# Two-layer hybrid trunk: the next layer's modulation moved from accumulations on DVE, ACT and POOL to float32r products on PE, and two sets of transpositions issued one tile later

## The chip, the core and the metric

The kernel runs on one core of a Trainium2 chip. The metric is the device time of one execution in microseconds; for each kernel the median of three runs is given. One further execution was taken by the hardware profiler, and all rows below come from that one. The engines are named as in the profile: PE (matrix products; PEld is its loading of weights), DVE (vector), ACT (scalar), POOL (GpSimd) and SP, whose queue issues nearly all transfers.

## What is computed

Two layers of a trunk are run over nine tiles of 128 tokens: one tile of context and eight latent tiles. Cut to what matters here:

```python
mod = jax.nn.silu(c) @ w_ada[l] + b_ada[l]          # for c_ctx and for c: two rows of 3 x 1024
shift, scale, gate = jnp.split(mod, 3, axis=-1)
h = rms_norm(x, p['norm_pre']) * (1 + scale) + shift
u = h @ p['w_in']                                   # 1024 -> 2952 columns: four branches and their gates
qa = rms_norm(gq, p['gqa_q_norm']); ka = rms_norm(gk, p['gqa_k_norm'])   # GQA, then rotary on both
cq = rms_norm(mcq, p['mla_q_norm']); ckv = rms_norm(mckv, p['mla_kv_norm'])   # MLA
...                                                 # attention A and C, scans B and D
y = x + gate * rms_norm(concat(o_a, o_b, o_c, o_d) @ p['w_out'], p['norm_post'])
```

The modulation of a layer is a product of two vectors with a matrix of 1024 x 3072. Everything is float32. A large product is made of three float32r products: both operands are split into a rounded part (`hi`) and the rest (`lo`), and hi x hi, hi x lo and lo x hi are added up in PSUM.

## The kernel before, in words

A layer runs through its projections first, one group of columns after another: LV, SM, MG, XBC, GQA, MLA, the second MLA projection (UQ) and QK. `proj_tok` (SM, GQA, MLA) loads eight slices of weights with `load_w` (a transfer into `wst`, a rounding cast to `whi` on DVE, a subtraction to `wlo` on POOL) and then gives each of the nine token tiles 24 products into one PSUM tile `psP`, of which there are four. `proj_T` (MG, XBC, QK) has columns as output rows, three stretches of 384 tokens each. After each tile `consume` is called: for GQA (`cons_gqa`) ACT squares, DVE reduces, POOL makes the reciprocal root, DVE scales (which frees `psP`), POOL and DVE apply the rotary factors, and PE transposes the result `r` into `gT`, which ACT copies out. `cons_mla` does the like with `z` and `mT`.

Within layer 0's projections a generator, `ada_steps`, makes the modulation that is still missing: the gate of layer 0 and shift, scale and gate of layer 1, as eight halves of 512 columns. A half takes eight steps, one for each 128 rows of `w_ada`; 72 calls of `next(steps_[0])` spread them over the projections from SM to QK. Layer 1 has the same projections without any such steps. Before the change a step loads 128 x 512 weights into `ast` (two buffers) and adds them, times one number for each partition, into `acc`, once for each of the two conditioning vectors: on DVE as one instruction (L176), or for one vector of a gate half on ACT (`pr`) and POOL (L174). PE then adds up the partitions of `acc`: with `acc` as weights and a 2-column `pick` as moving operand for shift and scale (L189), or the other way round for the gate (L183). `acc` has one buffer.

The order of instructions on each engine is not that of the code. A scheduler goes through the program with a model of time and lets each engine take what the model holds to be ready; each engine then runs its list strictly in that order and waits where the model was wrong.

Of the kernel before, what the change touches and what calls it, by code (L numbers as in the profile page):

```python
# [8 lines left out]
F32 = mybir.dt.float32  # L9
# [25 lines left out]
def hybrid_trunk_kernel(ctx: ExitStack, tc: tile.TileContext, a):  # L35
# [35 lines left out]
    dve.tensor_tensor(out=cch[:, :, 2:4], in0=cc, in1=cch[:, :, 0:2], op=ALU.subtract)  # L71
    sel = const.tile([4, 2], F32, name="sel")
    sp.dma_start(out=sel, in_=a["sel"])
# [3 lines left out]
    pool.memset(zero, 0.0)  # L77
    pick = const.tile([128, 2, 2], F32, name="pick")
    pool.memset(pick, 0.0)
    for r in range(2):  # L80
        pool.memset(pick[:, r, r:r + 1], 1.0)
    ident = const.tile([128, 128], F32, name="ident")
# [64 lines left out]

    def ada_rows(p, k, hi, lo):
        pe.matmul(p[0:4, :], lhsT=cch[:, k, :], rhs=hi, start=(k == 0), stop=False, skip_group_check=True)
        pe.matmul(p[0:2, :], lhsT=cch[:, k, 0:2], rhs=lo, start=False, stop=False, skip_group_check=True)  # L150

    def ada_put(mod, half, part, ac, sc, l):
        p = psD("adaT")
        for k in range(4):
            pe.matmul(p[:, 2 * k:2 * k + 2], lhsT=mod[:, k * 128:(k + 1) * 128], rhs=sel, start=(k == 0), stop=(k == 3),
                      skip_group_check=True)
        ada_cols(p, half * 4, 4, part, ac, sc, l)

    def ada_steps(l, parts, wpool, ac, sc, d_gate):

        for part, half in parts:
            o = part * D + half * 512
            acc = wpool.tile([128, 2, 512], F32, name="acc", tag="acc", bufs=1)
            for k in range(KD):
                st = wpool.tile([128, 512], F32, name="ast", tag="ast", bufs=2)
                sp.dma_start(out=st, in_=a["w_ada"][l, k * 128:(k + 1) * 128, o:o + 512])
                for r in range(2):
                    c = cc[:, k, r:r + 1]
                    if k == 0:
                        act.activation(out=acc[:, r, :], in_=st, func=AF.Identity, scale=c)  # L170
                    elif r and part == 2:
                        pr = wpool.tile([128, 512], F32, name="pr", tag="pr", bufs=1)
                        act.activation(out=pr, in_=st, func=AF.Identity, scale=c)
                        pool.tensor_tensor(out=acc[:, r, :], in0=acc[:, r, :], in1=pr, op=ALU.add)  # L174
                    else:
                        dve.scalar_tensor_tensor(out=acc[:, r, :], in0=st, scalar=c, in1=acc[:, r, :], op0=ALU.mult, op1=ALU.add)  # L176
                yield
            p = psC("ada")
            if part == 2:
                gr = wpool.tile([2, 512], F32, name="gr", tag="gr", bufs=1)  # L180
                sp.dma_start(out=gr, in_=a["b_ada"][l, o:o + 512].partition_broadcast(2))
                for r in range(2):
                    pe.matmul(p[0:2, :], lhsT=pick[:, r, :], rhs=acc[:, r, :], start=(r == 0), stop=(r == 1), skip_group_check=True)  # L183
                dve.tensor_tensor(out=gr, in0=p[0:2, :], in1=gr, op=ALU.add)
                sp.dma_start(out=d_gate[:, half * 512:half * 512 + 512], in_=gr)
            else:
                for k in range(4):
                    for r in range(2):
                        pe.matmul(p[:, 2 * k:2 * k + 2], lhsT=acc[:, r, k * 128:(k + 1) * 128], rhs=pick[:, r, :],  # L189
                                  start=(k + r == 0), stop=(k + r == 4), skip_group_check=True)  # L190
                ada_cols(p, half * 4, 4, part, ac, sc, l)
            yield

# [75 lines left out]
    def proj_tok(l, hh, hl, wpool, off, n, consume, rows=iter(())):  # L269
        ws = [load_w(a["w_in"][l, k * 128:(k + 1) * 128, off:off + n], n, wpool) for k in range(KD)]  # L270
        next(rows, None)
        next(rows, None)
        for t in range(T):
# [12 lines left out]
    def proj_T(l, hh, hl, wpool, off, nct, consume, after=None):  # L286
# [92 lines left out]
    for l in range(L):  # L379
# [83 lines left out]
        with st1:  # L463
# [134 lines left out]
            def cons_gqa(t, p):  # L598
# [52 lines left out]
            def cons_mla(t, p):  # L651
# [23 lines left out]
                pool.tensor_tensor(out=kr, in0=kr, in1=r[:, 0:32], op=ALU.add)  # L675
                tp = psD("mT")
                pe.transpose(tp[:, 0:128], z[:, 0:128], ident)
                pe.transpose(tp[0:64, 128:256], z[:, 128:192], ident)
                pe.transpose(tp[:, 256:384], z[:, 192:320], ident)
                s = slice(t * 128, (t + 1) * 128)  # L680
                act.copy(c1h[:, s], tp[:, 0:128])
                dve.tensor_tensor(out=c1l[:, s], in0=tp[:, 0:128], in1=c1h[:, s], op=ALU.subtract)
                act.copy(c2s[0:64, s], tp[0:64, 128:256])
                dve.tensor_tensor(out=c2s[64:128, s], in0=tp[0:64, 128:256], in1=c2s[0:64, s], op=ALU.subtract)
                s = slice(kt * 128, (kt + 1) * 128)
                act.copy(ckh[:, s], tp[:, 256:384])
                dve.tensor_tensor(out=ckl[:, s], in0=tp[:, 256:384], in1=ckh[:, s], op=ALU.subtract)

# [663 lines left out]
def _constants(np):  # L1352
# [16 lines left out]
    def rope(rot):  # L1369
# [17 lines left out]
        "bm": (hd[:, None] == (np.arange(256) // 64)[None, :]).astype(np.float32),  # L1387
        "sel": np.tile(np.eye(2, dtype=np.float32), (2, 1)),
        "hm": (hd[:, None] == np.arange(4)[None, :]).astype(np.float32),
# [91 lines left out]
```

## Time and profile before

| | |
|---|---|
| three runs, median | 1841.7 us (1835.44 to 1841.74) |
| the profiled execution | 1836.28 us, its span 1834.5 us |
| busy in the span | PE 1718.5, PEld 1312.8, DVE 1177.2, ACT 859.9, POOL 729.2 us |
| PE clock granted, mean | 0.973 of full speed |
| layer 0's projections, SM to QK | 102.68 to 423.20 us |
| layer 1's projections, SM to QK | 1014.58 to 1296.20 us |

Times inside the trace count from the first instruction. Busy time of PE is the time in which at least one product is under way, and products overlap, so it says little about how much PE could still take; the distance between two starts says more. The two stretches at the end of the table hold the same projections of the two layers; they begin at the first product of SM (128x296) and end at the first product of the attention that follows (L1102).

### The profile page before, as it was taken

The page shows a single profiled execution, that of the slowest core. Times are in us where ns is not written, and L with a number is a line of the kernel's source. Part 1 is how long each engine was busy: PE and PEld are TensorE (multiplying, and loading weights), DVE is VectorE, ACT ScalarE, POOL GpSimd, SP SyncE. Part 2 cuts the span into 40 slices and gives each one's busy share as a digit, 9 for nine tenths or more (in the row PEclk, how much of TensorE's full clock was granted, in tenths as well). Part 3 has the DMA queues.
Part 4 walks back from the last instruction along what each step waited for, and adds up shares of the span by engine and source line. Part 5 has one row for each costly group of instructions (what it writes and reads, how often), then busy time and mean ns, then how long its engine had stood idle before and what let it go on. Part 6 is the DMA issues. An engine that isn't in the chain of part 4 may idle for free.

```text
span 1834.5 us, 25155 instructions
## 1 busy us (share of the span) xinstructions
PE 1718.5 (94%) x8200; PEld 1312.8 (72%) x8200; DVE 1177.2 (64%) x2297; ACT 859.9 (47%) x1907; POOL 729.2 (40%) x909
## 2 busy tenths in 40 slices
PE   8999998998998998999999999999999899899998
PEld 2787977896665666656887999889666666565676
DVE  5738887647877886772453447543776788678223
ACT  4634422434654765673442162132465467567322
POOL 3633149824343543330343323871434354333011
PEclk9999988999989999999999999999998999999999
DMA  8435353413323321142433333231442332114243
GB/s 296 138 117 156 113 168 103 129 63 119 115 77 85 90 79 47 41 144 86 138 129 104 102 94 91 60 102 37 122 116 76 81 88 83 50 36 149 87 137 115
DMA packets 179684, 190.99 MB, mean 104 GB/s; under 512 B 29406, under 2 KB 140720, under 8 KB 179552
## 3 DMA queue, kind: packets, MB, share of 16 engines
q1 hardware_dynamic: 174208, 179.11, 32.1%
q10 hardware_dynamic: 5344, 10.26, 1.7%
q8 instruction: 65, 1.06, 0.3%
q14 instruction: 67, 0.55, 0.1%
HBM read 141.00 MB, written 48.30 MB: 103 GB/s over the span
## 4 chain that ended last, share of the span: by engine, by line
PE 54%; DVE 17%; DMA 11%; POOL 7%; issue 5%; ACT 4%; SPq 1%; ACTq 0%; POOLq 0%; DVEq 0%
PE psP L267 19%; PE op L267 8%; PE st L1102 5%; PE po L1118 5%; DMA ast<-in_w_ada_dram 2%; PE mx L755 2%; DMA wst<-in_w_in_dram 2%; DVE mx L756 2%; DVE Pl L1110 2%; PE po L1114 1%; DVE acc L176 1%; DMA R<-d_rec 1%; POOL wlo L261 1%; DVE d_DT L1023 1%; PE go L931 1%
## 5 line engine op out<-in xcount | busy, mean ns | idle before, releaser
L756 DVE TENSOR_REDUCE mx<-mx 128x1 f32<-128x512 f32 (+2 forms) x400 | 224.6, 582 | 92.2 <-PE mx L755 90.6
L267 PE MATMUL psP<-whi,hh 128*128 128x512 f32 (+2 forms) x576 | 202.6, 363 | 6.1 <-DVE whi L257 3.7
L267 PE MATMUL psP<-wlo,hh 128*128 128x512 f32 (+2 forms) x576 | 202.8, 361 | 2.1 <-POOL wlo L261 1.9
L267 PE MATMUL psP<-whi,hl 128*128 128x512 f32 (+2 forms) x576 | 187.5, 359 | 0.1
L261 POOL TENSOR_TENSOR wlo<-wst,whi 128x512 fp32r<-128x512 f32 (+3 forms) x106 | 130.6, 1240 | 137.9 <-DVE whi L257 79.0
L267 PE MATMUL psP<-hh,whi 128*128 128x384 f32 x480 | 163.1, 340 | 4.7 <-DVE whi L257 3.8
L1102 PE MATMUL st<-QA,KA 128*128 128x512 f32 (+1 forms) x336 | 164.0, 488 | 0.6 <-DVE Pl L1110 0.4
L267 PE MATMUL psP<-hl,whi 128*128 128x384 f32 x480 | 160.2, 336 | 0.0
L267 PE MATMUL psP<-hh,wlo 128*128 128x384 f32 x480 | 155.0, 337 | 0.1
L1110 DVE TENSOR_TENSOR Pl<-st,Ph 128x512 fp32r<-128x512 f32 x160 | 109.7, 686 | 65.9 <-ACT st L1108 64.2
L1107 ACT ACTIVATE Ph<-st 128x512 fp32r<-128x512 f32 x160 | 95.5, 597 | 107.5 <-PE st L1102 99.1
L1117 ACT ACTIVATE P<-st 128x512 f32<-128x512 f32 (+1 forms) x176 | 99.8, 567 | 79.1 <-PE st L1102 67.1
L1102 PE MATMUL st<-QB,KB 66*128 66x512 f32 (+3 forms) x336 | 133.0, 401 | 0.0
L267 PEld LDWEIGHTS psP<-whi,hh 128*128 128x128 f32 x576 | 110.3, 193 | 20.3 <-DVE whi L257 5.2
L267 PEld LDWEIGHTS psP<-wlo,hh 128*128 128x128 f32 x576 | 110.4, 193 | 17.9 <-POOL wlo L261 5.3
L267 PEld LDWEIGHTS psP<-whi,hl 128*128 128x128 f32 x576 | 108.5, 192 | 12.4 <-DVE hl L226 0.3
L1102 PEld LDWEIGHTS st<-QA,KA 128*128 128x128 f32 x336 | 65.4, 195 | 49.8 <-issue 39.3
L267 PEld LDWEIGHTS psP<-hh,whi 128*128 128x128 f32 x480 | 90.1, 188 | 12.0 <-DVE whi L257 5.5
L1102 PE MATMUL st<-QB,KA 96*128 96x512 f32 (+1 forms) x168 | 93.2, 555 | 2.1 <-ACT P L1117 1.8
L1108 ACT ACTIVATE st<-st 128x512 f32<-128x512 f32 x160 | 94.8, 592 | 0.0
L1118 PE MATMUL po<-P,vm 128*65 128x512 f32 (+1 forms) x176 | 88.7, 586 | 5.9 <-ACT P L1117 3.4
L1144 POOL TENSOR_TENSOR gt<-gt,R 128x512 f32<-128x512 f32 (+1 forms) x24 | 26.6, 1106 | 166.0 <-DMA R<-d_rec 162.3
(369 smaller groups left out, 4325.2 us busy)
## 6 DMA issues: line engine op xcount, KB each, us to landing
ast<-in_w_ada_dram SPq DMA_DIRECT2D x96, 256.0 KB
wst<-in_w_in_dram SPq DMA_DIRECT2D x64, 256.0 KB
wost<-in_w_out_dram SPq DMA_DIRECT2D x16, 512.0 KB
d_xs<-d_xb SPq DMA_DIRECT2D x32, 192.0 KB
ot<-d_oT SPq DMA_DIRECT2D x18, 320.0 KB
d_tok<-vv SPq DMA_DIRECT2D x18, 256.0 KB
d_gt<-gg SPq DMA_DIRECT2D x24, 192.0 KB
g_qk<-d_qk SPq DMA_DIRECT2D x36, 128.0 KB
```

What stands on the lines that cost most here:

```text
L176: dve.scalar_tensor_tensor(out=acc[:, r, :], in0=st, scalar=c, in1=acc[:, r, :], op0=ALU.mult, op1=ALU.add)
L261: eng.tensor_tensor(out=lo[:, 0:n], in0=st[:, 0:n], in1=hi[:, 0:n], op=ALU.subtract)
L267: pe.matmul(p, lhsT=lt, rhs=rh, start=(first and i == 0), stop=(last and i == n - 1))
L755: pe.matmul(p[:, 0:n], lhsT=lt_m[:, s], rhs=rh_m[:, o:o + n], start=True, stop=True)
L756: dve.tensor_reduce(out=mx[:, t, i:i + 1], in_=p[:, 0:n], axis=AX.X, op=ALU.max)
L1102: anchors["pe"] = pe.matmul(sp_[:, 0:nq], lhsT=kx[:, ks], rhs=qx[:, qs], start=(i == 0), stop=(i == len(spasses) - 1))
L1107: act.activation(out=Ph[:, 0:nq], in_=sp_[:, 0:nq], func=AF.Exp, scale=scale)
L1108: anchors["act"] = act.activation(out=sp_[:, 0:nq], in_=sp_[:, 0:nq], func=AF.Exp, scale=scale)
L1110: anchors["dve"] = dve.tensor_tensor(out=Pl[:, 0:nq], in0=sp_[:, 0:nq], in1=Ph[:, 0:nq], op=ALU.subtract)
L1117: anchors["act"] = act.activation(out=P[:, 0:nq], in_=sp_[:, 0:nq], func=AF.Exp, scale=scale)
L1118: pe.matmul(po[0:65, 0:nq], lhsT=v[:, kt, vi, :], rhs=P[:, 0:nq], start=(j == 0), stop=last, skip_group_check=True)
L1144: pool.tensor_tensor(out=g[:, 0:nq], in0=g[:, 0:nq], in1=R[:, 0:nq], op=ALU.mult)
```

## The change

A step of `ada_steps` now splits the 128 x 512 weights: ACT rounds them to `ahi`, DVE or POOL (in turn) subtracts to `alo`, and PE multiplies both with the conditioning vectors as weights of 4 and 2 columns, adding up in one PSUM tile over the eight steps (`ada_rows`, L145 and L146 of the new kernel). The products of a step are issued one step later. A half ends with a copy of the four rows to `mod` on ACT, and one step later with four small float32 products (`adaT`, shift and scale) or one float32 product of 512 columns (gate, L181, in which a fifth row adds the bias). `acc`, `pr`, `pick` and their sums are gone. In `proj_tok`, what `consume` returns is called one tile later; `cons_gqa` and `cons_mla` return the transpositions and the copies behind them.

```diff
@@ ada_steps
-            acc = wpool.tile([128, 2, 512], F32, name="acc", tag="acc", bufs=1)
+            p = psC("ada")
+            behind = None
             for k in range(KD):
                 st = wpool.tile([128, 512], F32, name="ast", tag="ast", bufs=2)
                 sp.dma_start(out=st, in_=a["w_ada"][l, k * 128:(k + 1) * 128, o:o + 512])
-                for r in range(2):
-                    c = cc[:, k, r:r + 1]
-                    if k == 0:
-                        act.activation(out=acc[:, r, :], in_=st, func=AF.Identity, scale=c)
-                    elif r and part == 2:
-                        pr = wpool.tile([128, 512], F32, name="pr", tag="pr", bufs=1)
-                        act.activation(out=pr, in_=st, func=AF.Identity, scale=c)
-                        pool.tensor_tensor(out=acc[:, r, :], in0=acc[:, r, :], in1=pr, op=ALU.add)
-                    else:
-                        dve.scalar_tensor_tensor(out=acc[:, r, :], in0=st, scalar=c, in1=acc[:, r, :], op0=ALU.mult, op1=ALU.add)
+                hi = wpool.tile([128, 512], F32R, name="ahi", tag="ahi", bufs=2)
+                act.copy(hi, st)
+                lo = wpool.tile([128, 512], F32R, name="alo", tag="alo", bufs=2)
+                (pool if k % 2 else dve).tensor_tensor(out=lo, in0=st, in1=hi, op=ALU.subtract)
+                if behind:
+                    ada_rows(p, *behind)
+                behind = k, hi, lo
                 yield
-            p = psC("ada")
+            ada_rows(p, *behind, True)
+
+            mod = wpool.tile([5, 512], F32, name="mod", tag="mod", bufs=1)
+            act.copy(mod[0:4, :], p[0:4, :])
             if part == 2:
...
+                sp.dma_start(out=mod[4:5, :], in_=a["b_ada"][l:l + 1, o:o + 512])
+            yield
+            if part == 2:
+                p = psC("ada")
+                pe.matmul(p[0:2, :], lhsT=sel, rhs=mod, start=True, stop=True)
+                act.copy(mod[0:2, :], p[0:2, :])
+                sp.dma_start(out=d_gate[:, half * 512:half * 512 + 512], in_=mod[0:2, :])
             else:
...
+                ada_put(mod[0:4], half, part, ac, sc, l)
@@ proj_tok
-            consume(t, p)
+
+            last, rest = rest, consume(t, p)
+            if last is not None:
+                last()
             for _ in range(2 - t % 2):
                 next(steps_[0], None)
+        if rest is not None:
+            rest()
@@ cons_gqa (cons_mla alike)
-                tp = psD("gT")
-                for i in range(3):
-                    pe.transpose(tp[:, i * 128:(i + 1) * 128], r[:, i * 128:(i + 1) * 128], ident)
-                act.copy(qT[:, :, t * 128:(t + 1) * 128], tp[:, 0:256].rearrange("p (a b) -> p a b", b=128))
-                act.copy(kT[:, kt * 128:(kt + 1) * 128], tp[:, 256:384])
+
+                def rest():
+                    tp = psD("gT")
+                    ...
+                return rest
```

The order of the built programs differs only between the first tiles of SM and the start of the attention in layer 0: on PE the first 356 and the last 4887 instructions are the same, one for one, by what they do, layer 1's projections with their transpositions among them.

The first place is DVE at the start of GQA in layer 0. `whi` are the casts of GQA's weights, `yc` the end of XBC's convolution, `ss` the reductions of the first two GQA tiles, from which their scaling `z` comes. Before:

```order
L122 SCALAR_TENSOR_TENSOR ac<-ac,np_c 128x8
L176 SCALAR_TENSOR_TENSOR acc<-ast,cc,acc 128x512
L578 SCALAR_TENSOR_TENSOR yc<-xpad,yc 128x1156
L257 CAST whi<-wst 128x512
L176 SCALAR_TENSOR_TENSOR acc<-ast,cc,acc 128x512 x2
L257 CAST whi<-wst 128x512
L176 SCALAR_TENSOR_TENSOR acc<-ast,cc,acc 128x512 x10
L606 TENSOR_REDUCE ss_2429<-sq 128x6
L606 TENSOR_REDUCE ss_2487<-sq 128x6
L609 TENSOR_TENSOR z<-psP,ss_2429 128x384
```

And now:

```order
L574 SCALAR_TENSOR_TENSOR yc<-xpad,cw,yc 128x1156 x2
L250 CAST whi<-wst 128x512
L167 TENSOR_TENSOR alo<-ast,ahi 128x512
L250 CAST whi<-wst 128x512
L577 SCALAR_TENSOR_TENSOR yc<-xpad,yc 128x1156
L605 TENSOR_REDUCE ss_2509<-sq 128x6
L605 TENSOR_REDUCE ss_2569<-sq 128x6
L608 TENSOR_TENSOR z<-psP,ss_2509 128x384
```

Twelve accumulations of the modulation stood around the last cast and ahead of the first reduction; one subtraction is left there, ahead of the last cast.

The second place is PE at the end of QK, the last projection; `mx` are products for the maxima of the attention that follows, `st` its first scores. Before:

```order
L267 MATMUL psP<-hl,whi 128x384
L755 MATMUL mx<-KA_3633,QA_3635 128x256
L267 MATMUL psP<-hh,wlo 128x384
L183 MATMUL ada<-acc,pick 2x512
L1102 MATMUL st<-QA_3635,KA_3633 128x128
L1102 MATMUL st<-QB_3636,KB_3634 128x128
L755 MATMUL mx<-KA_3633,QA_3635 128x512 x2
```

And now:

```order
L260 MATMUL psP<-hh,wlo 128x384
L762 MATMUL mx<-KA_3797,QA_3799 128x512
L145 MATMUL ada<-ahi,cch 4x512
L146 MATMUL ada<-alo,cch 2x512
L1109 MATMUL st<-QA_3799,KA_3797 128x128
L1109 MATMUL st<-QB_3800,KB_3798 128x128
L762 MATMUL mx<-KA_3797,QA_3799 128x256
L181 MATMUL ada<-mod,sel 2x512
```

The last pair of the modulation has come into PE's list, and its closing product (L181, where L183 stood) has moved behind the first scores of the attention.

## Rows read from the trace of the kernel before

**Rows 1.** The profile's page: busy time, share of the span and instructions of PE.

```profile
PE 1718.5 (94%) x8200; PEld 1312.8 (72%) x8200; DVE 1177.2 (64%) x2297; ACT 859.9 (47%) x1907; POOL 729.2 (40%) x909
```

**Rows 2.** Layer 0's projections by stretch: us, busy PE, PEld, DVE, ACT, POOL, clock.

```profile
102.68:136.10 33.42, 31.70 (x221) 29.57 (x220) 14.05 (x29) 12.36 (x30) 13.55 (x12) 1.00 0.45 130
136.10:231.56 95.46, 90.66 (x509) 83.47 (x508) 77.56 (x113) 43.72 (x72) 28.47 (x36) 1.00 0.47 138
231.56:297.01 65.45, 61.23 (x278) 50.07 (x277) 55.10 (x70) 13.97 (x34) 40.01 (x37) 0.92 0.47 137
297.01:349.80 52.79, 46.77 (x268) 43.39 (x267) 33.13 (x62) 20.21 (x81) 45.59 (x76) 0.90 0.35 102
349.80:423.20 73.40, 73.18 (x391) 64.81 (x390) 42.29 (x77) 25.74 (x59) 30.02 (x30) 1.00 0.30 94
sum 320.52, PE 303.55 PEld 271.31 DVE 222.12 ACT 116.00 POOL 157.65; mean PE 60.71 PEld 54.26 DVE 44.42 ACT 23.20 POOL 31.53
```

**Rows 3.** The same five stretches in layer 1, and their sum.

```profile
1014.58:1044.00 29.42, 29.42 (x217) 29.38 (x217) 8.10 (x24) 5.23 (x18) 6.98 (x10) 1.00 0.26 77
1044.00:1130.70 86.70, 86.16 (x497) 82.35 (x496) 50.92 (x78) 38.50 (x64) 18.92 (x29) 1.00 0.31 95
1130.70:1182.60 51.90, 51.50 (x237) 42.29 (x236) 35.99 (x42) 10.80 (x32) 40.96 (x43) 1.00 0.26 72
1182.60:1224.40 41.80, 39.56 (x250) 37.83 (x249) 19.78 (x53) 13.27 (x69) 29.87 (x63) 1.00 0.29 79
1224.40:1296.20 71.80, 69.88 (x383) 64.58 (x382) 30.41 (x62) 19.39 (x47) 17.30 (x22) 1.00 0.21 66
sum 281.62, PE 276.52 PEld 256.43 DVE 145.21 ACT 87.20 POOL 114.04; mean PE 55.30 PEld 51.29 DVE 29.04 ACT 17.44 POOL 22.81
```

**Rows 4.** Whom PE waited for in layer 0's projections: us in total, times, longest.

```profile
PE gT L629 <- DVE r L626: 4.8, 4, 2.6
PE psP L267 <- DVE whi L257: 4.5, 6, 1.5
PE ada L189 <- DVE acc L176: 3.5, 1, 3.5
PE ada L183 <- DVE acc L176: 2.2, 2, 1.7
```

**Rows 5.** In order of time, DVE and ACT at the start of GQA (start, us).

```profile
255.22 0.50 ACT L604 ACTIVATE sq<-psP 128x384 f32<-128x384 f32 x1
260.54 1.42 DVE L176 SCALAR_TENSOR_TENSOR acc<-ast,cc,acc 128x512 f32<-128x512 f32 x2 [0.87 <-DMA ast<-in_w_ada_dram]
261.87 1.00 DVE L606 TENSOR_REDUCE ss<-sq 128x6 f32<-128x384 f32 x2
```

**Rows 6.** PE in order of time, where products of the modulation stand (start, us).

```profile
26.16 1.05 PE L155 MATMUL adaT<-sel,mod 4*128 4x2 f32 x8
...
38.19 0.39 PE L149 MATMUL ada<-ahi,cch 128*4 128x512 f32 x1
38.42 0.40 PE L267 MATMUL psP<-whi,hh 128*128 128x512 f32 x1
...
300.22 0.95 PE L189 MATMUL ada<-pick,acc 128*128 128x2 f32 x8
...
327.15 1.02 PE L183 MATMUL ada<-acc,pick 128*2 128x512 f32 x2
```

**Rows 7.** What writes `ada` on PE: records, ns min/median/max, first and last start.

```profile
L189 PE MATMUL ada<-pick,acc x64: 165/251/374, 182.4 to 300.9; 128*128 128x2 f32 x64
L183 PE MATMUL ada<-acc,pick x16: 591/592/592, 127.9 to 422.7; 128*2 128x512 f32 x16
```

**Rows 8.** What reads `ast`: records, ns min/median/max, first and last start.

```profile
L176 DVE SCALAR_TENSOR_TENSOR acc<-ast,cc,acc x84: 735/751/1828, 111.0 to 374.1; 128x512 f32<-128x512 f32 x84
L140 DVE TENSOR_TENSOR alo<-ast,ahi x12: 670/691/694, 5.2 to 33.0; 128x512 fp32r<-128x512 f32 x12
```

**Rows 9.** Whom DVE waited for in layer 0's projections.

```profile
DVE acc L176 <- DMA ast<-in_w_ada_dram: 16.1, 18, 2.7
```

More of the change, by code (lines that the diff above doesn't have):

```diff
@@ L71, in hybrid_trunk_kernel @@
     dve.tensor_tensor(out=cch[:, :, 2:4], in0=cc, in1=cch[:, :, 0:2], op=ALU.subtract)
-    sel = const.tile([4, 2], F32, name="sel")
+    sel = const.tile([5, 2], F32, name="sel")
     sp.dma_start(out=sel, in_=a["sel"])
@@ L77, in hybrid_trunk_kernel @@
     pool.memset(zero, 0.0)
-    pick = const.tile([128, 2, 2], F32, name="pick")
-    pool.memset(pick, 0.0)
-    for r in range(2):
-        pool.memset(pick[:, r, r:r + 1], 1.0)
     ident = const.tile([128, 128], F32, name="ident")
@@ L146, in ada0, with ada_rows @@
         return load.ins
-    def ada_rows(p, k, hi, lo):
+    def ada_rows(p, k, hi, lo, last=False):
         pe.matmul(p[0:4, :], lhsT=cch[:, k, :], rhs=hi, start=(k == 0), stop=False, skip_group_check=True)
-        pe.matmul(p[0:2, :], lhsT=cch[:, k, 0:2], rhs=lo, start=False, stop=False, skip_group_check=True)
+        pe.matmul(p[0:2, :], lhsT=cch[:, k, 0:2], rhs=lo, start=False, stop=last, skip_group_check=True)
     def ada_put(mod, half, part, ac, sc, l):
@@ L154, in ada_put @@
         for k in range(4):
-            pe.matmul(p[:, 2 * k:2 * k + 2], lhsT=mod[:, k * 128:(k + 1) * 128], rhs=sel, start=(k == 0), stop=(k == 3),
+            pe.matmul(p[:, 2 * k:2 * k + 2], lhsT=mod[:, k * 128:(k + 1) * 128], rhs=sel[0:4], start=(k == 0), stop=(k == 3),
                       skip_group_check=True)
@@ L166, in ada_steps @@
                 sp.dma_start(out=st, in_=a["w_ada"][l, k * 128:(k + 1) * 128, o:o + 512])
-                for r in range(2):
-                    c = cc[:, k, r:r + 1]
-                    if k == 0:
-                        act.activation(out=acc[:, r, :], in_=st, func=AF.Identity, scale=c)
-                    elif r and part == 2:
-                        pr = wpool.tile([128, 512], F32, name="pr", tag="pr", bufs=1)
-                        act.activation(out=pr, in_=st, func=AF.Identity, scale=c)
-                        pool.tensor_tensor(out=acc[:, r, :], in0=acc[:, r, :], in1=pr, op=ALU.add)
-                    else:
-                        dve.scalar_tensor_tensor(out=acc[:, r, :], in0=st, scalar=c, in1=acc[:, r, :], op0=ALU.mult, op1=ALU.add)
+                hi = wpool.tile([128, 512], F32R, name="ahi", tag="ahi", bufs=2)
@@ L179, in ada_steps @@
             if part == 2:
[L180 to L185, printed above, removed]
-            else:
[L187 to L191, printed above, removed]
@@ L192, in ada_steps @@
-            yield
+                sp.dma_start(out=mod[4:5, :], in_=a["b_ada"][l:l + 1, o:o + 512])
[5 more added lines that the diff above has]
+                sp.dma_start(out=d_gate[:, half * 512:half * 512 + 512], in_=mod[0:2, :])
+            else:
+                ada_put(mod[0:4], half, part, ac, sc, l)
     PARTS = [(p, h) for p in (1, 0, 2) for h in range(2)]
@@ L272, in proj_tok @@
         next(rows, None)
+        rest = None
         for t in range(T):
@@ L626, in cons_gqa @@
                 dve.tensor_tensor(out=r, in0=r, in1=sq, op=ALU.add)
-                tp = psD("gT")
-                for i in range(3):
-                    pe.transpose(tp[:, i * 128:(i + 1) * 128], r[:, i * 128:(i + 1) * 128], ident)
-                act.copy(qT[:, :, t * 128:(t + 1) * 128], tp[:, 0:256].rearrange("p (a b) -> p a b", b=128))
-                act.copy(kT[:, kt * 128:(kt + 1) * 128], tp[:, 256:384])
+                def rest():
+                    tp = psD("gT")
+                    for i in range(3):
+                        pe.transpose(tp[:, i * 128:(i + 1) * 128], r[:, i * 128:(i + 1) * 128], ident)
+                    act.copy(qT[:, :, t * 128:(t + 1) * 128], tp[:, 0:256].rearrange("p (a b) -> p a b", b=128))
+                    act.copy(kT[:, kt * 128:(kt + 1) * 128], tp[:, 256:384])
+                return rest
             proj_tok(l, hh, hl, wp, G_GQA, 512, cons_gqa)
@@ L675, in cons_mla, with rest @@
                 pool.tensor_tensor(out=kr, in0=kr, in1=r[:, 0:32], op=ALU.add)
[L676 to L687, printed above, removed]
+                def rest():
+                    tp = psD("mT")
+                    pe.transpose(tp[:, 0:128], z[:, 0:128], ident)
+                    pe.transpose(tp[0:64, 128:256], z[:, 128:192], ident)
+                    pe.transpose(tp[:, 256:384], z[:, 192:320], ident)
+                    s = slice(t * 128, (t + 1) * 128)
+                    act.copy(c1h[:, s], tp[:, 0:128])
+                    dve.tensor_tensor(out=c1l[:, s], in0=tp[:, 0:128], in1=c1h[:, s], op=ALU.subtract)
+                    act.copy(c2s[0:64, s], tp[0:64, 128:256])
+                    dve.tensor_tensor(out=c2s[64:128, s], in0=tp[0:64, 128:256], in1=c2s[0:64, s], op=ALU.subtract)
+                    s = slice(kt * 128, (kt + 1) * 128)
+                    act.copy(ckh[:, s], tp[:, 256:384])
+                    dve.tensor_tensor(out=ckl[:, s], in0=tp[:, 256:384], in1=ckh[:, s], op=ALU.subtract)
+                return rest
             proj_tok(l, hh, hl, wp, G_MLA, 352, cons_mla)
@@ L1387, in _constants @@
         "bm": (hd[:, None] == (np.arange(256) // 64)[None, :]).astype(np.float32),
-        "sel": np.tile(np.eye(2, dtype=np.float32), (2, 1)),
+        "sel": np.concatenate([np.eye(2), np.eye(2), np.ones((1, 2))]).astype(np.float32),
         "hm": (hd[:, None] == np.arange(4)[None, :]).astype(np.float32),
```

## The prediction

> **What bounds the kernel now.** I read the page first: PE is busy for 94% of the span [rows 1]. As products overlap, that number does not say that PE is full, so the next view is busy time by stretch. The two layers run the same projections, layer 0 with the modulation's steps among them and layer 1 without. Layer 0 takes 320.52 us and layer 1 281.62 us [rows 2, 3]: the steps cost 38.9 us now. By stretch the difference is 4.0 us in SM, 8.8 in MG and XBC, 13.6 in GQA, 11.0 in MLA and 1.6 in UQ and QK. PEld, whose loads are hidden behind the products, is busy for 256 of 282 us in layer 1, so there PE is close to what it can take. In layer 0 DVE is busy for 222 us, in layer 1 for 145; in GQA PE idles for 4.2 us and in MLA for 6.0, and there alone the granted clock falls, to 0.92 and 0.90 of full speed [rows 2]. The levels are 2.4 and 1.2 GHz, so a mean of 0.92 over 65.45 us is about 10.5 us at the lower one, and 0.90 over 52.79 us as much. The waits that end last there are for `r`, for `whi` and for `acc` [rows 4]. One of them is plain in order of time: ACT has squared the first GQA tile at 255.2 us, but DVE reduces it at 261.9, since accumulations that wait for `ast` stand ahead in its list [rows 5]; the four `psP` tiles stay taken until then.
>
> **What the change takes away.** On PE two kinds of product go. L183 has 16 records and L189 has 64 [rows 7]; the trace lists a float32 product as two records, so these are 8 and 32 instructions. Two records of L183 take 1.02 us and eight of L189 0.95 [rows 6]: 16 x 0.51 = 8.2 us and 64 x 0.119 = 7.6, together 15.8 us of PE's own time. So of the 38.9 us, 38.9 - 15.8 = 23.1 are waits and lost clock. DVE loses 84 accumulations of 0.751 us (63 us), ACT 44 scalings and POOL 28 additions; that alone is worth nothing to the end unless PE waits less.
>
> **What it adds on PE.** A half has eight steps, each with two float32r products of 512 columns: 8 x 8 x 2 = 128. The first layer-0 modulation issues this very form (L149), and the product behind it starts 38.42 - 38.19 = 0.23 us later [rows 6]. That is what one of the 128-column products costs too: only four columns of weights make it no cheaper. 128 x 0.23 = 29.4 us. Four gate halves end with a float32 product of 512 columns, in the form of L183: 4 x 1.02 = 4.1 us. Four halves of shift and scale end with the small products of L155: 4 x 1.05 = 4.2 us [rows 6]. Together 37.7 us, against 15.8 taken away: PE's list grows by 21.9 us.
>
> The Trainium skill bears on the dearest term: "TensorE: Matmul & The Clock Gate", section "Back-to-back issue gap", gives a sustained 131 ns for a 512-column product in a stream with its loads of weights. By it the 128 products would be 16.8 us, an estimate from that page, and the sum 12.6 us smaller. The row shows 0.23 us, so the row is used, and the page's figure gets no chance of its own.
>
> **What it adds elsewhere.** ACT gets 64 roundings and twelve small copies. ACT is busy for 116 of 320 us [rows 2], so this is hidden unless something behind it in ACT's list is due: ACT's casts wait for `ast` now, and the copies and squares that free `psP` are queued behind them. DVE and POOL get 32 subtractions each. DVE's took 0.691 us [rows 8], 22 us in all, so DVE comes out 41 us lighter. POOL's count hardly changes (28 additions gone). SP's transfers of `ast` stay 64, with two buffers; each buffer is now freed by the subtraction. Of the bias, the transfer to two rows becomes one to one row. The last product, L181, has moved behind the attention's first scores and waits for a copy on ACT; I take that into the remainder below.
>
> **The transpositions.** From the attention of layer 0 on PE's list is the same as before, so in layer 1 the later issue moves nothing: it is worth nothing there. In layer 0 the scheduler had placed the transpositions by readiness already. Counting the products between a GQA tile's last one and its `gT`, at their distances between starts, tiles three to nine had 13.5 to 23.5 us before and have 10.8 to 20.8 now: they stand no later, but DVE, which is late with `r`, has less ahead of it. I give this half of the 4.8 us of waits [rows 4], and nothing more.
>
> **The sum.** Layer 0's projections after the change are layer 1's 281.6, plus 37.7 for PE, plus a remainder X of waits beyond those of layer 1. Below, X can be -5.1: layer 1 has 281.62 - 276.52 = 5.1 us of PE idle, which pairs could fill [rows 3]. Above, without new waits, it is the 23.1 of today. By stretch I take 2 of SM's (there the steps follow each other as fast as `ast` arrives, now as before), 2.5 in MG and XBC, 2 in GQA (the block of accumulations is gone, and with it the waiting for `acc` and most of the low clock), 4 in MLA, where `whi` and `r` remain late, nothing in UQ and QK, and -4.5 for holes filled: X = 6, nearer the lower end since DVE, which three of the four waits name, loses 41 us. 281.6 + 37.7 + 6 = 325.3, against 320.5: 4.8 us more. The profiled execution took 1836.28 us, 1.8 more than its span, and becomes 1841.1. It lies 5.4 below the median of the three runs; carried over to the median, 1841.7 + 4.8 = 1846.5 us.
>
> By stretch: SM +3 us, MG and XBC +3, GQA -5, MLA -1, UQ and QK +5. In the last PE is never idle for long (73.18 of 73.40), so eleven pairs come to it as they are.
>
> **The rivals.** A measurement of this kernel can tell about 0.5%, 9.2 us, from no change.
>
> *Holes filled, faster.* The pairs are products that need no `psP` tile, so PE can take them while it waits for one. For a gain of 9.2 us X must fall below -8.0, which means that also waits inside layer 1's pattern go, and no clock is lost. At X = -9 the window takes 310.3 us and the kernel 1831.5. For it: GQA and MLA idle now. Against it: PE's list alone is 319.3 us beside layer 1's. Chance 0.10.
>
> *A wait at each pair, slower.* PE's list has 64 pairs at fixed places, each behind a transfer, a cast and a subtraction, where before PE met the modulation in eight places. DVE waited 16.1 us for `ast` in 18 places, 0.9 us each [rows 9]; if PE's places come as early and nothing fills them, X is 6 + 16 = 22 and the time 1862.5. It decides from X = 10.4 on. For it: an accumulation takes 0.735 to 1.828 us [rows 8], so what the scheduler counts on is missed by up to a microsecond. Against it: one late pair moves PE's whole list, so that the next is no longer early, and DVE has fewer of these instructions. Chance 0.25.
>
> A rule of the Trainium skill speaks for this rival: in "SBUF — State Buffer", section "SBUF: two separate sides", a DVE instruction with two SBUF inputs and one of POOL hold a shared pair of ports in turn, each blocking the other for a whole instruction. Both subtractions of the change are of that kind. The spread of L176 agrees; what an `alo` costs against POOL is in no row.
>
> *The transpositions help nothing.* If `r` stays as late as it is, the 4.8 us and the clock that falls behind them (5.3 us in MLA at half speed) stay: about 6.5 us more than taken, X = 12.5, 1853. For it: the transpositions stand no later than before. Against it: the lighter DVE. Chance 0.13.
>
> *The forecast*, within 9.2 us either way: chance 0.52. Its own range is X from 0 to 10, 1840 to 1851 us.
>
> **Range and chances.** For 8 in 10 I go down to X = -6 (1834.5 us), which leaves out most of the first rival, and up to X = 20 (1860.5), which leaves out the worst of the second: 1834 to 1861 us. Faster by over 0.5% is the first rival, 0.10; slower the second and third, 0.25 + 0.13 = 0.38; within 0.5% the forecast, 0.52.
>
> **What would show it.** Right: DVE busy near 180 us from SM to the first scores instead of 222, PE's pairs 0.23 us apart, GQA shorter than 65.45 us, the last stretch some 5 us longer, the first GQA reduction within a microsecond or two of its square, and everything from the attention on unchanged. Wrong: PE waiting for `alo` or `ahi` for more than 5 us in all; waits for `r` of over 4 us; a clock below 0.95 in GQA or MLA; pairs that cost less than 0.2 us; or a changed time outside this window.

## The result, and the profile after

The changed kernel takes 1855.88 us (median of four runs, 1854.17 to 1857.73), the one before in the same rounds 1839.78: a ratio of 1.0095, with a 95% interval of 1.0072 to 1.0118. It is slower by 0.95%, inside the range that was given and beyond the time that was forecast.

The profiled execution has a span of 1855.4 us, 20.9 more than before. The first view is again busy time by stretch, in the same five stretches of layer 0 (columns as in [rows 2]):

```profile
103.15:139.98 36.83, 35.79 (x240) 31.79 (x239) 9.36 (x27) 12.51 (x32) 9.89 (x10) 1.00 0.49 137
139.98:246.69 106.71, 100.24 (x545) 87.94 (x543) 60.20 (x89) 49.81 (x86) 31.90 (x37) 0.98 0.41 120
246.69:308.49 61.80, 59.44 (x268) 44.84 (x267) 43.42 (x50) 17.91 (x45) 51.70 (x48) 1.00 0.38 109
308.49:363.60 55.11, 50.68 (x290) 44.92 (x289) 26.24 (x61) 21.07 (x84) 40.85 (x72) 0.94 0.42 122
363.60:441.12 77.52, 77.28 (x412) 67.18 (x410) 36.71 (x71) 26.24 (x62) 24.07 (x27) 1.00 0.31 97
sum 337.97, PE 323.43 PEld 276.67 DVE 175.94 ACT 127.54 POOL 158.40; mean PE 64.69 PEld 55.33 DVE 35.19 ACT 25.51 POOL 31.68
```

The window has grown from 320.5 to 338.0 us, by 17.4 of the 20.9. Against [rows 2], SM is 3.4 us longer, MG and XBC 11.3, GQA 3.7 shorter, MLA 2.3 longer, UQ and QK 4.1 longer. DVE is 46 us lighter and the wait for `acc` is gone; GQA now runs at the full clock. The same stretches of layer 1 are where they were, 281.62 then and now:

```profile
sum 281.82, PE 276.51 PEld 256.58 DVE 147.71 ACT 87.15 POOL 114.32; mean PE 55.30 PEld 51.32 DVE 29.54 ACT 17.43 POOL 22.86
```

Whom PE waited for in the window (us, times, longest), to be held against [rows 4]:

```profile
PE psP L260 <- DVE whi L250: 4.5, 6, 1.5
PE ada L145 <- ACT ahi L165: 3.0, 4, 2.0
PE gT L630 <- DVE r L625: 2.4, 2, 2.0
PE psP L260 <- POOL wlo L254: 1.8, 3, 0.9
PE cums L508 <- DVE av L500: 1.2, 1, 1.2
```

At the pairs themselves PE waits 3.0 us in all. The wait for `whi` is what it was, that for `r` has halved, and `wlo` and `av` are new. A pair in order of time (start, us):

```profile
429.75 0.39 PE L145 MATMUL ada<-ahi,cch 128*4 128x512 f32 x1
429.98 0.39 PE L146 MATMUL ada<-alo,cch 128*2 128x512 f32 x1
430.21 0.39 PE L762 MATMUL mx<-KA,QA 128*128 128x512 f32 x1
```

The products of the pairs stand 0.23 us apart; over all 128 the median is 0.234, which makes 30.0 us. The Trainium skill's "TensorE: Matmul & The Clock Gate", section "Back-to-back issue gap", has 131 ns for a 512-column product in a sustained stream; this trace does not agree.

The first GQA tile in order of time:

```profile
269.14 0.50 ACT L603 ACTIVATE sq<-psP 128x384 f32<-128x384 f32 x1
269.68 0.55 DVE L605 TENSOR_REDUCE ss<-sq 128x6 f32<-128x384 f32 x1 [4.28 <-ACT sq L603]
```

DVE now reduces half a microsecond after the square, where it came 6.65 us after it [rows 5]. The longest wait for `r` comes later, at one of GQA's last tiles, with MLA's weights being made ready (PE, DVE, POOL and SP together, start in us):

```profile
310.99 1.23 SPq L248 DMA_DIRECT2D wst<-in_w_in_dram  x2
313.37 0.34 DVE L250 CAST whi<-wst 128x352 fp32r<-128x352 f32 x1 [2.71 <-DMA wst<-in_w_in_dram]
313.63 0.95 DVE L618 TENSOR_TENSOR r<-z,ropes 128x384 f32<-128x384 f32 x1
314.12 1.26 POOL L254 TENSOR_TENSOR wlo<-wst,whi 128x352 fp32r<-128x352 f32 x1
314.96 0.62 DVE L250 CAST whi<-wst 128x352 fp32r<-128x352 f32 x1
315.34 1.36 POOL L167 TENSOR_TENSOR alo<-ast,ahi 128x512 fp32r<-128x512 f32 x1
315.50 1.61 DVE L625 TENSOR_TENSOR r<-r,sq 128x384 f32<-128x384 f32 x1
317.17 0.55 PE L630 MATMUL gT<-ident,r 128*128 128x128 f32 x3 [1.97 <-DVE r L625]
```

This shows how PE comes to wait. A cast waits 2.71 us for its weights with `r` queued behind it, and then the last step of `r` takes 1.61 us, beside a subtraction `alo` on POOL; the one of the tile before took 0.55. A slow step of this kind is not new, though: in the kernel before it took up to 1.63 us. PE waits 1.97 us for it, and its clock falls:

```profile
157.00:160.50 3.50, 3.50 (x14) 2.90 (x13) 0.21 (x2) 0.95 (x3) 0.00 (x0) 0.53 0.33 112
316.50:324.50 8.00, 7.33 (x27) 6.31 (x28) 2.53 (x7) 1.78 (x4) 6.13 (x7) 0.57 0.58 176
```

These two are nearly all of the window's time at 1.2 GHz: 2 x (1 - 0.53) x 3.5 + 2 x (1 - 0.57) x 8 = 10.2 us, half of the 21 before.

That the `alo` beside it is what stretches `r` is what the Trainium skill would have, in "SBUF — State Buffer", section "SBUF: two separate sides": DVE with two SBUF inputs and POOL take turns on a shared pair of ports, each for a whole instruction. The row agrees, with 1.06 us; one pair of rows does not show that it is the port.

### The profile page after: what moved, and what is told of

Same layout as the page of the kernel before. It is cut to its first block, busy times and chain, and to the rows that moved or that the text cites. A ratio compares the mean times of both kernels' runs of the same rounds, so it can differ in the third digit from the quotient of the medians.

```text
span 1855.4 us, 25323 instructions
## 1 busy us (share of the span) xinstructions
PE 1741.0 (94%) x8288; PEld 1318.6 (71%) x8288; DVE 1133.2 (61%) x2241; ACT 872.7 (47%) x1939; POOL 729.4 (39%) x910
## 4 chain that ended last, share of the span: by engine, by line
PE 33%; DVE 7%; DMA 5%; POOL 3%; issue 2%; ACT 2%; SPq 0%; ACTq 0%; POOLq 0%; DVEq 0%
PE psP L260 12%; PE op L260 9%; PE st L1109 3%; PE po L1125 2%; PE mx L762 1%; DVE mx L763 1%; DMA R<-d_rec 1%; POOL ss L103 1%; PE po L1121 1%; POOL sq L621 1%; DVE Pl L1117 1%; DMA wst<-in_w_in_dram 1%; PE go L938 1%; PE po L1119 0%; PE po L1120 0%
## 5 line engine op out<-in xcount | busy, mean ns | idle before, releaser
L250 DVE CAST whi<-wst 128x512 fp32r<-128x512 f32 (+3 forms) x114 | 72.7, 650 | 50.9 <-DMA wst<-in_w_in_dram 33.4
```

Source lines behind the costliest of these rows:

```text
L250: dve.tensor_copy(hi[:, 0:n], st[:, 0:n])
```

## The experiments

Two theories were set against each other. **List**: PE's list has grown by 21.9 us, and that is what arrives. **Chain**: what arrives comes from feeding the pairs, 64 times a transfer, a rounding and a subtraction, whose places in the lists of SP, ACT, DVE and POOL delay what the projections need. Beside them stood the question what the later transpositions are worth. "Window" is the time of the five stretches in the one profiled execution of a kernel; ratios are to the kernel before, in the same rounds on the same chip (its median was 1839.8 us in the changed kernel's rounds and 1836.0 to 1837.6 in those of the others, so medians of different rows are compared by their ratios).

| kernel | window, us | median, us | ratio, 95% interval |
|---|---|---|---|
| before | 320.5 | 1839.8 | |
| changed | 338.0 | 1855.9 | 1.0095 [1.0072, 1.0118] |
| e1, modulation only | 334.1 | 1853.3 | 1.0096 [1.0068, 1.0124] |
| e2, transpositions only | 320.0 | 1834.8 | 0.9992 [0.9972, 1.0011] |
| e3, no chain | 323.4 | 1848.1 | 1.0044 [1.0023, 1.0066] |
| e4, few pairs | 329.6 | 1845.1 | 1.0040 [1.0021, 1.0059] |
| e5, transfers without splits | 345.7 | 1868.3 | 1.0178 [1.0141, 1.0215] |
| e6, splits without transfers | 327.1 | 1851.1 | 1.0082 [1.0050, 1.0114] |
| e7, subtractions on DVE | 329.7 | 1846.2 | 1.0057 [1.0034, 1.0080] |
| e8, third `ast` | 344.1 | 1866.9 | 1.0171 [1.0138, 1.0203] |
| e9, neither chain nor pairs | 298.8 | 1813.0 | 0.9877 [0.9857, 0.9897] |
| e10, roundings on DVE too | 329.5 | 1855.1 | 1.0110 [1.0095, 1.0125] |
| e11, two halves on PE | 320.3 | 1837.2 | 1.0010 [0.9999, 1.0020] |
| e12, transfers on ACT's queue | 331.0 | 1853.9 | 1.0091 [1.0070, 1.0111] |

The time outside the window is 1514.0 us of the span in the kernel before and between 1508.1 (e9) and 1523.5 (e8) in the others, although the instructions there are nearly the same; the last section shows one such place. So causes are read from the windows, and a difference of less than some 4 us between two windows is not used.

**e1 and e2: the two parts apart.**

```diff
# e1: the changed kernel, transpositions in their own tile
-            last, rest = rest, consume(t, p)
-            if last is not None:
-                last()
+            now = consume(t, p)
+            if now is not None:
+                now()
```

> The changed kernel with the transpositions issued in their own tile again, so that only the modulation's part of the change is left. If the later transpositions are worth nothing (they stood no later in PE's list than before): 1856 us, within 3, and GQA and MLA together 117 us as in the changed kernel. If they are what made GQA shorter: the 4.8 us of waits for r and the clock behind them come back, 1861 to 1868 us, GQA and MLA together 122 to 129.

e2 is the kernel before with the changed kernel's `proj_tok`, `cons_gqa` and `cons_mla`.

> The kernel before with the later transpositions alone; the modulation stays on DVE, ACT and POOL. If they are worth nothing: 1840 us, within 3. If they take away waits for r and the low clock in GQA and MLA: 1829 to 1835 us, PE's waits for r below 2 us in all where there were 4.8.

e1 has the ratio of the changed kernel, 1.0096; its window is 3.9 us shorter, with GQA and MLA at 116.5 us against 116.9. In e2 the window and its waits are those of before (sum of the five stretches, and PE's wait for `r`):

```profile
sum 320.02, PE 303.42 PEld 271.18 DVE 223.87 ACT 116.32 POOL 158.76; mean PE 60.68 PEld 54.24 DVE 44.77 ACT 23.26 POOL 31.75
```

```profile
PE gT L637 <- DVE r L632: 4.6, 3, 2.6
```

The median of e2, 1834.8 us, lies where the other case was expected, but the kernel before took 1836.7 in the same rounds. The later transpositions are worth nothing that can be measured, in either company. What halved the wait for `r` is the modulation's part of the change: e1, without the later transpositions, has 2.0 us of it. That DVE's lighter load did it is not shown: e4 below, with as light a DVE as the changed kernel, has 5.5 us of this wait.

**e3, e4 and e9: chain and pairs, each out and both out.**

```diff
# e3: one slice, split once, feeds all pairs
-                st = ...; sp.dma_start(out=st, ...); hi = ...; act.copy(hi, st); lo = ...
+                if not one:
+                    ...                                # the same, once
+                    one[:] = hi, lo
+                hi, lo = one
# e4: only the first and the last step of a half multiply
-                if behind:
+                if behind and k == 1:
                     ada_rows(p, *behind)
# e9: both
```

> The changed kernel, but all 64 pairs use one pair of slices that is loaded and split once: 63 transfers, 63 roundings and 63 subtractions are left out, the 128 products stay. If PE's list sets the end (theory: list): the window from SM to the attention's first scores loses only what PE waits directly at the pairs, some 4 us, and comes to 330 to 336 us; the kernel takes 1848 to 1854. If the chain that feeds the pairs delays the rest through SP's queue, ACT, DVE and POOL (theory: chain): the remainder falls from 19 to 6 us or less, the window to 325 or less and the kernel to 1843 or less.

> The changed kernel with the products of the first and the last step of each half alone: 96 of the 128 are left out; transfers, roundings and subtractions all stay. If PE's list sets the end (list): 96 x 0.234 = 22.5 us less, window 315.5 us, kernel 1833, within 4. If the chain delays (chain): less than half of that, 1845 us or more.

> No chain and few pairs at once: one pair of slices is loaded and split once, and only the first and the last step of each half multiply; 63 transfers, roundings and subtractions and 96 products are left out. Each alone took the window from 338.0 to 323.4 (no chain) and to 329.6 us (few pairs). If PE's list sets the end as soon as the chain is gone: another 22.5 us less than 323.4, 301 us, within 3. If the two add up as they did alone: 315 us. If the projections have a bound of their own in MG and XBC: 318 or more.

The sums of the five stretches, of e3:

```profile
sum 323.44, PE 315.69 PEld 273.71 DVE 137.62 ACT 94.50 POOL 109.49; mean PE 63.14 PEld 54.74 DVE 27.52 ACT 18.90 POOL 21.90
```

of e4:

```profile
sum 329.56, PE 303.12 PEld 266.95 DVE 174.97 ACT 126.97 POOL 155.35; mean PE 60.62 PEld 53.39 DVE 34.99 ACT 25.39 POOL 31.07
```

and of e9:

```profile
sum 298.84, PE 293.94 PEld 263.05 DVE 140.30 ACT 94.84 POOL 108.21; mean PE 58.79 PEld 52.61 DVE 28.06 ACT 18.97 POOL 21.64
```

| window, us | chain in | chain out | the chain costs |
|---|---|---|---|
| all 128 products | 338.0 | 323.4 | 14.6 |
| 32 products | 329.6 | 298.8 | 30.8 |
| 96 products cost | 8.4 | 24.6 | |

Neither theory holds alone. Without the chain the list is nearly the time: 96 x 0.234 = 22.5 us, and 24.6 arrive. With it, only 8.4 us of them do, and the chain's own cost is 14.6 us where PE has all its products and 30.8 where it has few. So the pairs do fill holes, but 16 us of holes that the chain has made. PE's idle time, the sum less its busy time, shows them: with the chain it is 14.5 us with all products and 26.4 with few, without it 7.8 and 4.9. The ratios of the whole kernels have the same form: by them the chain costs 0.5% with all products and 1.6% with few. One expectation was missed: the window of e3 is where the chain's theory had it, but its median, 1848.1 us, is where the list's had it, as 5.4 us more than in the changed kernel pass outside the window.

How the chain makes one is seen in e4, in XBC. `xpad` are the copies on ACT that free `psP`; ACT in order of time:

```profile
198.64 0.62 ACT L165 CAST ahi<-ast 128x512 fp32r<-128x512 f32 x1 [7.92 <-POOL alo L167]
...
204.11 0.62 ACT L165 CAST ahi<-ast 128x512 fp32r<-128x512 f32 x1 [1.94 <-DMA ast<-in_w_ada_dram]
204.63 0.26 ACT L563 COPY xpad<-psP 128x128 f32<-128x128 f32 x1
204.79 0.38 ACT L564 COPY xpad<-psP 128x256 f32<-128x256 f32 x1
```

and whom PE waited for there:

```profile
PE psP L260 <- ACT xpad L564: 4.3, 1, 4.3
```

Roundings that wait for a subtraction on POOL, and then for a transfer, stand ahead of the copies; PE waits 4.3 us for the second one, which frees its `psP`. In the changed kernel neither wait, ACT's for POOL's `alo` nor PE's for `xpad`, is in the lists, so this shows how the chain can make a hole, not where the changed kernel's are.

In e3 not all of the stretches fall alike: MLA goes from 55.1 to 47.9 us, MG and XBC only from 106.7 to 104.1. In the latter 4.4 us are one wait for `whi`, with no chain in it: DVE's cast stands behind `gg`, for which DVE waits 4.71 us until ACT has loaded three tables, of 1.28 us each, for two other activations and for its own.

**e5, e6 and e8: which link.**

```diff
# e5: transfers as in the changed kernel, split once
# e6: one transfer, 64 splits of the same slice
# e8: a third slice; the closing tile takes its turn in the ring
-                st = wpool.tile([128, 512], F32, name="ast", tag="ast", bufs=2)
+                st = wpool.tile([128, 512], F32, name="ast", tag="ast", bufs=3)
-            mod = wpool.tile([5, 512], F32, name="mod", tag="mod", bufs=1)
+            mod = wpool.tile([5, 512], F32, name="mod", tag="ast", bufs=3)
```

> The changed kernel with the 64 transfers of the weights left in and 63 roundings and subtractions left out; the 128 products use one pair of slices. Without the whole chain the window from SM to the first scores took 323.4 us, with it 338.0. If the transfers cost it (their places in SP's queue, ahead of the projections' weights, and the traffic): 333 us or more. If the places of the roundings and subtractions on ACT, DVE and POOL cost it: 323 to 327. If it needs both (a rounding that stands in ACT's list and waits for a late transfer, with PSUM copies behind it): 323 to 327 here, and the same without the transfers.

> The counterpart: one slice is loaded once, and all 64 roundings and subtractions are made from it; 63 transfers are left out, the 128 products stay. If the transfers cost the 14.6 us: window 323 to 327 us. If the places on ACT, DVE and POOL do: 333 or more. If it needs both: 323 to 327.

> The changed kernel with a third buffer for the slices (the closing tile mod takes its turn in the same ring, so the memory is the same). If roundings that wait for a late transfer cost the time: ACT waits less for ast than the 44 us of the changed kernel, the window comes to 326 to 333 us and the kernel to 1844 to 1851. If not: 338 within 3, 1853 to 1859.

e6 has a window of 327.1 us: with every rounding and subtraction in place but no transfer to wait for, 10.9 of the 14.6 us are gone; the 3.7 that are left are too few to be used. That fits "the transfers cost it" and "it needs both", and speaks against the places alone. The sum of its five stretches:

```profile
sum 327.14, PE 318.05 PEld 273.99 DVE 178.03 ACT 127.81 POOL 159.34; mean PE 63.61 PEld 54.80 DVE 35.61 ACT 25.56 POOL 31.87
```

e5 does not separate those two as it was meant to. With nobody to read the slices, the transfers run ahead and crowd MG and XBC, the second stretch here:

```profile
139.78:262.27 122.49, 106.89 (x538) 94.36 (x539) 49.53 (x81) 40.65 (x68) 20.04 (x30) 0.89 0.55 164
```

DVE's casts waited 33.3 us for `wst` in the window, 22.5 in e3, and PE waited 9.1 us at once for `whi`; GQA and MLA, with the crowd behind them, are as short as in e3 or nearly (58.8 and 50.3 us). In this run, transfers that come too early thus cost more than late ones.

e8 went against what was expected. ACT's waits for `ast` fell from 44.1 to 28.6 us, and the window grew to 344.1, most of it in GQA (66.5) and in UQ and QK (81.8). The scheduler made another order of it, with the closing tile bound to the slices' ring, and new waits for `z` (4.2 and 3.6 us). So the sum of ACT's waits does not measure the cost; whether a shorter wait saves anything in the same order is not shown. Each version here is scheduled anew, so the order can be a part of any difference between two windows; how large a part is not known.

**e7, e10 and e12: who does the work.**

```diff
# e7
-                (pool if k % 2 else dve).tensor_tensor(out=lo, in0=st, in1=hi, op=ALU.subtract)
+                dve.tensor_tensor(out=lo, in0=st, in1=hi, op=ALU.subtract)
# e10: e7, and
-                act.copy(hi, st)
+                dve.tensor_copy(hi, st)
# e12: e10, and
-                sp.dma_start(out=st, in_=...)
+                act.dma_start(out=st, in_=...)
```

> The changed kernel with all 64 subtractions on DVE. If POOL's subtractions, of 1.3 us each, keep DVE off its operands or stand ahead of the projections' own on POOL, the window shrinks by 3 to 10 us, to 328 to 335, and DVE's casts whi are no longer stretched; if not, it stays at 338, within 3, or grows with DVE's 22 us.

> The changed kernel with all subtractions on DVE and the roundings there too, so that nothing of a step stands in ACT's or POOL's list; DVE gets 64 roundings of some 0.42 us, 27 us more. With the subtractions alone moved, the window was 329.7 us. If what was left of the chain's cost is ACT's list, where a rounding waits for a late transfer (32 us in all there) with the copies out of PSUM behind it: 323 to 327 us. If it is the late transfer itself, whoever waits for it: 328 to 334, with the waits for ast now on DVE. If DVE's load is the cost: 335 or more.

> Roundings and subtractions on DVE as in e10, and the 64 transfers of the slices issued from ACT's queue, so that none of them stands between the projections' weights in SP's. The window was 329.5 us with them on SP. If their places in SP's queue are what the transfers cost: 323 to 327 us. If it is the late arrival or the traffic: 328 to 332. If ACT, which then waits for a free slice ahead of its copies out of PSUM, pays for it: 335 or more.

e7's window is 329.7 us, 8.3 less than the changed kernel's, and its ratio is the lowest of the versions that compute the whole modulation on PE, with an interval that still touches the changed kernel's: the gain is shown in the window, not beyond doubt in the kernel's time. Of the 8.3, some 3.4 are the clock, which is at half for 3.4 us where it was for 10.2. The sum of its stretches, and the lines of its waits for the pairs and for `r`:

```profile
sum 329.67, PE 318.55 PEld 273.82 DVE 182.68 ACT 127.26 POOL 116.34; mean PE 63.71 PEld 54.76 DVE 36.54 ACT 25.45 POOL 23.27
```

```profile
PE ada L145 <- ACT ahi L165: 2.5, 2, 1.9
...
PE gT L630 <- DVE r L625: 0.6, 2, 0.4
```

Adding up how much longer each DVE instruction of the window took than the shortest of its line and shape gives 32.3 us in the changed kernel, 24.5 here and 15.9 in e3. DVE does 32 subtractions more and is stretched by 8 us less. This agrees with what was cited of shared ports; that a step also has a shorter way, 0.69 us instead of 1.30, and that POOL's own list is shorter, is not told apart from it. The casts `whi` of 128x512 are still stretched, by 4.3 us in all where it was 7.8. The kernel before has 43.4 us by the same count, with its accumulations on POOL, so stretching as such is not what the change added.

In e10 and e12 the window stays where e7 had it, 329.5 and 331.0 us. So neither ACT's list nor the transfers' places in SP's queue shows as what is left of the cost. They are not excluded: a gain can be hidden under DVE's load, 207.3 us in e10 against 182.7 in e7, and in e12 under ACT's waits for transfers of its own queue, 12.6 us in one place. Against what was expected of the late transfer, DVE waits only 10.1 us for `ast` in e10. The medians of both are no better than the changed kernel's; in e10's profiled execution UQ and QK of layer 1 take 5.2 us more than in the changed kernel's, part of the time at the lower clock.

**e11: two halves of eight.**

```diff
+            if (l, part, half) not in ON_PE:      # ON_PE = ((1, 1, 1), (1, 0, 0))
+                yield from ada_sums(...)          # accumulations as before
+                continue
```

> Two halves of the modulation of eight, the second of the scale and the first of the shift, which fall into XBC's end and GQA, as products on PE with their subtractions on DVE; the other six as accumulations as before; transpositions one tile later. PE's list: 16 pairs x 0.468 + 2 x 1.05 = 9.6 us for 2 x 1.9 = 3.8, 5.8 us more than before. If the accumulations in GQA alone cause its waits and the 10 us at half the clock: GQA 56 to 60 us instead of 65.45, the window 313 to 318 instead of 320.5, the kernel 3 to 7 us under the one before. If the chain's cost comes with each pair: 14.6 x 2/8 = 3.7 us back, the kernel within 3 us of the one before.

The window is 320.3 us, the ratio 1.0010: no better than the kernel before. GQA falls to 59.3 us, as expected, but MG and XBC take 4.7 us more than before, and MLA, at 53.9 us, is no shorter. The gain is real in its stretch and given back in others. The window is above the 313 to 318 us that were expected of a gain, and the kernel is within 3 us of the one before, as was expected if the chain's cost comes with each pair. No version that computes the whole result is measurably faster than the kernel before.

## Why the prediction was right where it was, and where it was not

**What PE's list costs** was right: 0.234 us a product where 0.23 was taken, and without the chain the window is 323.4, against 281.6 + 37.7 = 319.3. So was what comes off the other engines (DVE 176 us, 180 predicted), and that layer 1 stays as it was. By stretch SM (+3.4, predicted +3), GQA (-3.7, -5) and the last (+4.1, +5) came near; MG and XBC (+11.3, +3) and MLA (+2.3, -1) did not. One of the prediction's own signs of being wrong appeared: the clock is 0.94 in MLA, below the 0.95 that it named.

**The remainder X** was mis-sized. It was taken at 6, "nearer the lower end since DVE, which three of the four waits name, loses 41 us" (all four of [rows 4] name DVE), and is 338.0 - 281.6 - 37.7 = 18.7. X by stretch is what the stretch has over layer 1's and its own products (10, 18, 12, 13 and 11 pairs start in the five): SM 1.7, MG and XBC 9.5, GQA 3.2, MLA 5.1, UQ and QK -0.5. These add up to 19.1, as the last closing product, of 1.0 us, starts at 442.0 us, behind the window, and the pairs are taken at the measured 0.234 us a product. Two terms make most of the difference: MG and XBC, taken at 2.5, and the 4.5 us taken off for holes filled. Without the chain X is 4.1, so 6 would have been near if the chain cost nothing. The failing step is the one in which ACT's 64 roundings were "hidden", DVE counted as "41 us lighter" and POOL and the 64 transfers as hardly changed. The busy times were right: POOL 158.4 after, 157.7 before. What the step left out is that each split stands in an ordered list, behind a transfer and in front of something else: e6, with all splits and no transfers to wait for, has 10.9 us less. e7, with POOL's 32 subtractions moved away from beside DVE's work, has 8.3 less. The two overlap, as the whole chain is worth 14.6.

That the time lies inside the range is owed to the range's upper end, which was set for the second rival; the forecast itself was 4.8 us more, and 16.1 came (17.4 in the window). A slowing of over 0.5% had a chance of 0.38, less than the forecast's 0.52.

**The rivals.** "A wait at each pair" gave X = 22 and 1862.5 us, and by X the outcome lies nearer to it than to the forecast. Its place was wrong: PE waits 3.0 us at the pairs, not 16, and the rest comes at `whi`, `wlo`, `av` and `r` and as lost clock. "The transpositions help nothing" is what e1 and e2 show; but as half of the wait for `r` went with the accumulations, little of the time hangs on it. That pairs fill holes is seen in e4 and e9, but the holes are the chain's, and the gain that this rival forecast did not come even without the chain: e3 is at 1.0044. The forecast gave 10.4 as the X from which the kernel is slower by more than 0.5%; its range of 0 to 10 was too narrow for a term that no row showed.

**Open.** Which part of a late transfer's cost comes through whom is not settled: e6 leaves 10.9 us to the transfers' being there, e12 gives no sign of their places in SP's queue, e8 does not tell as its order is another, and e5 tells only of early ones. Of the 9.5 us in MG and XBC most stay without the chain, as waits of the projections' own casts in the order that the scheduler chose.

## What to carry to other kernels

Work that goes to the engine that is already full cost about its list time here (24.6 us for a list of 22.5) once nothing had to be prepared for it; price the preparation by its places in the ordered lists and by the transfers that it waits for there, not by the busy time of the engines. Taking out feeding and products singly and together tells their costs apart, which taking out one never does: here 14.6 and 8.4 us singly, 39.2 together. Where a gain in one stretch is real, look at the next one before it is counted.

## What the runs showed of the hardware

The same instructions in the same order can take nearly 10% longer in one execution than in another. UQ and QK of layer 1 stand unchanged in the changed kernel and in e6; the stretch in the changed kernel:

```profile
1242.17:1313.90 71.73, 69.82 (x384) 64.56 (x383) 31.53 (x62) 19.38 (x47) 17.29 (x22) 1.00 0.21 66
```

and in e6, whole and in the part where the clock was low:

```profile
1232.68:1311.36 78.68, 75.23 (x384) 68.61 (x383) 30.72 (x62) 19.36 (x47) 17.08 (x22) 0.91 0.19 60
...
1238.68:1247.68 9.00, 8.02 (x22) 5.61 (x23) 3.07 (x8) 1.22 (x5) 5.45 (x8) 0.50 0.34 104
```

In e6 PE had waited once for 2.48 us just ahead of the part at the low clock, in the changed kernel 0.93 us at that place:

```profile
1238.48 0.69 PE L265 MATMUL psP<-c1h,whi 128*128 128x384 f32 x1 [2.48 <-ACT qn L732]
```

2 x (1 - 0.91) x 78.68 = 14 us at 1.2 GHz cost 7 us. e5, e8 and e10 show the same in this stretch (77.0, 78.3 and 77.0 us), with 2.15 to 2.17 us of that wait. The longer wait does not decide it alone: e1 and e3 have 2.17 and 2.16 us of it, keep the full clock, and take 72.98 us. In e3:

```profile
1234.10 0.45 PE L265 MATMUL psP<-c1h,whi 128*128 128x384 f32 x1 [2.16 <-ACT qn L732]
...
1228.61:1301.59 72.98, 69.84 (x384) 64.56 (x383) 31.14 (x62) 19.38 (x47) 17.19 (x22) 1.00 0.20 65
```

In the other eight traces the wait is 0.93 to 0.96 us and the clock stays full. So the low clock came only behind the longer wait, in four of six; what decides among these six stays open. Far from the change, it is worth as much as most of the differences that were looked for.

DVE and POOL hold each other up from both sides. In the changed kernel, at the start of GQA's weights:

```profile
259.40 2.41 POOL L167 TENSOR_TENSOR alo<-ast,ahi 128x512 fp32r<-128x512 f32 x1
260.58 1.51 DVE L250 CAST whi<-wst 128x512 fp32r<-128x512 f32 x1
```

The subtraction takes 1.30 us at the median and the cast 0.43; here the subtraction, which began beside the end of `yc`, takes 2.41 and the cast beside it 1.51.
